# Twelve early gate/up units instead of eight, and GpSimd's FFN sums and low parts moved to VectorE, in a one-core transformer layer

## The chip, the core and the metric

One core of a Trainium2 chip runs the whole layer. TensorE (PE in the profile) multiplies, with its weight loads listed apart as PEld; VectorE (DVE), ScalarE (ACT) and GpSimd (POOL) do the work on elements; SyncE (SP) issues most DMAs. The metric is the device time of one execution in microseconds (us). The time before is the median of three runs.

## The reference

```
h = modulate(rms_norm(x, g_ffn1), sh_f1, sc_f1)
x = x + 0.5 * gt_f1 * ((silu(h @ w1_gu[gate]) * (h @ w1_gu[up])) @ w1_down)
h = modulate(rms_norm(x, g_mix), sh_m, sc_m);  z = h @ w_in     # two mixers: latent and grouped-query attention
x = x + gt_m * (concat(rms_norm(o_mla), rms_norm(o_gqa)) @ w_out)
h = modulate(rms_norm(x, g_ffn2), sh_f2, sc_f2)
x = x + 0.5 * gt_f2 * ((silu(h @ w2_gu[gate]) * (h @ w2_gu[up])) @ w2_down)
out = rms_norm(x, g_final)
```

All is float32, with 1024 tokens, a model width of 1024 and an FFN width of 2816. The nine vectors sh_*, sc_*, gt_* are the blocks of silu(c) @ w_ada + b_ada, each 1024 long.

## The kernel before

Every float32 operand of a matmul is split into a high part (ScalarE's cast, L105 or L461) and a low part (VectorE's subtraction, L106 or L462), and three matmuls on the parts replace one. So the FFNs are made of matmuls of 128x128 weights and 512 columns.

**Seven products.** Each FFN's gate/up projection uses a 2x2 block scheme with seven products instead of eight. The tokens are cut into two halves and the model width into two halves, which gives the blocks B11, B21 (first token half) and B12, B22 (second). `build` turns them into T1, T2, T3, T4 and the parts of B22, in eight steps (four 128-row chunks, two parts each); a step has four or five subtractions and low parts, of which GpSimd does one in the first part and three in the second. The weights come in 22 units (a gate and an up unit make a pair), each of four blocks A11, A12, A21, A22, streamed from DRAM, 1 MB a unit. `unit_specs` forms the sums S1 to S4 of the blocks: S1 and S3 on GpSimd, S2 and S4 on VectorE. A product is 12 matmuls (4 chunks, 3 terms).

**Early units.** A11xB11 and A12xB21 need the first token half alone. For the first NE units they run ahead of the rest, while the T blocks are still being built: the first NQ0 = 4 units in `early` (FFN1) or `early2` (FFN2), the others four at a time in `early_rest`. The weights of these two blocks come in transfers of their own (`first_spec`, one for a pair of units), and again with the unit. The result of A11xB11 (`c1`) and the first-half output (`ge_d`) go out to DRAM and come back in `run`. `run` then does five products for an early unit and seven for any other: A11, S2, S1, S3, A12, S4 and, one unit late, A22.

**What lies around the products.** `post` applies silu and the multiplication on the results, and `g_out` forms the sums S1 to S4 of the 512-wide results for the down projection, on GpSimd (L521), and stores them: names that begin with A on the SyncE queue, the others on GpSimd's. The down projection (`down`, L741 to L743) is again seven products, of 11 steps of 12 matmuls. Its first product takes the A12 results, loaded in three chunks.

**Streams and order.** `Stream.pump` splits the next weight blocks ahead of their use into a ring of nine units. After each product `tick` steps the background generators, pumps, and at `ada_rate` eighths of the ticks advances a second stream, `ada`: 56 steps that build seven of the nine modulation vectors, eight steps a vector. A step (L313) multiplies 128 rows of w_ada by c and adds them into the tile `acc`; there is one such tile at a time. When the eight steps of a vector are done, a generator sums `acc` over partitions with small matmuls (`mod_cols`, L328, or `mod_gate`, L342), and the next vector's memset waits for these. The rate is 0 in the early units of `run` and 5 in the others; what is left is done after it:

```
    ada.raw_pools["raw"] = (lambda: gup.tile([P, D], F32, tag="ada", name="ada", bufs=2), 2)
    ...
    ffn.run()
    while ada.i < len(ada.specs):
        ada.pump(1)
    bg.finish()
    gs.close()
    rs.close()
```

`gs.close()` gives back the pool of `acc`, `ada` and the results g; the tiles `gate` and x of the down projection take its place. PSUM tiles come from three pools of 3, 1 and 4 banks ("0", "1" and "2"), in rotation: in `run` by SIX = 0, 0, 0, 1, 2 low, 2 low; in `down` the eight accumulators take all banks, in the order 0, 0, 0, 1 for the first product and the four of pool 2 for the second.

The framework sets the order of each engine's queue when the program is built: code order counts first, but an instruction whose inputs it expects to be ready may go ahead of one that it expects to wait. On the chip each queue runs in its order.

Of the kernel before, what the change touches and what calls it, by code (L numbers as in the profile page):

```python
# [19 lines left out]
ALU = mybir.AluOpType  # L20
# [13 lines left out]
RING = 9  # L34
RAWB = 2
NQ0 = 4
NE = 8
TAIL = 3
YQ, YQ2, YL = 0, 1, 0
QB = 1  # L40
# [11 lines left out]
class Stream:  # L52
# [87 lines left out]
    def get(self, key):  # L140
        while key not in self.units:
            assert self.i <= self.where[key], key
            if self._next_is_block() and self.live >= RING:
                self.live -= self.freed
                self.freed = 0
                assert self.live < RING, key
            self._step()
        return self.units[key]
# [35 lines left out]
def encoder_layer(ctx: ExitStack, tc: tile.TileContext, a: dict, out: bass.AP):  # L184
    nc = tc.nc
# [10 lines left out]
    st = Stream(nc, rawp, ring)  # L196
# [17 lines left out]
    def t2(name, dt=F32):  # L214
        return tmp.tile([P, 512], dt, tag="t2", name=name, bufs=6)

    def small(n, name):
        return sm.tile([P, 16], F32, tag="small", name=name, bufs=20)[:, 0:n]
# [30 lines left out]
    g_d = {nm: dram.tile([P, NF // 2, 512], F32, name=f"g_{nm}") for nm in ("A11", "A12", "A22", "S1", "S2", "S3", "S4")}  # L249
    ge_d = dram.tile([NE // 2, P, 512], F32, name="ge_d")  # L250
    p1_d = dram.tile([NE, P, 512], F32, name="p1_d")
    gd = dram.tile([3, D], F32, name="gd")
# [27 lines left out]
    def ps1():  # L280

        if banks["pair"] is not None:
            p = banks["pair"][:, 512:1024]
            banks["pair"] = None
            return p
        kind = banks["kinds"][banks["n"] % len(banks["kinds"])]
        banks["n"] += 1
        if kind[0] == "2":
            p = ps2()
            if kind == "2":  # L290
                banks["pair"] = p
            return p[:, 0:512]
        return (p0p if kind == "0" else p1p).tile([P, 512], F32, tag="ps1", name="ps1")
# [122 lines left out]
    def unit_specs(i, u, early):  # L416

        src = a[f"w{i}_gu"][u // 2, u % 2]
        A = [slice(j * 512, (j + 1) * 512) for j in range(4)]
        tmps = {}  # L420

        def comb(nm, eng, x, y, op):
            def f(raw):
                tmps[nm] = sp.tile([P, 512], F32, tag="S", name="S")
                get = lambda v: tmps[v] if isinstance(v, str) else raw[:, A[v]]
                eng.tensor_tensor(tmps[nm], get(x), get(y), op=op)  # L426
            return f

        def blk(nm, v):
            if isinstance(v, str):  # L430
                return ((i, u, nm), None, lambda raw: tmps[v])
            return ((i, u, nm), A[v], None)

        direct = not early
        steps = [comb("S1", nc.gpsimd, 2, 3, ALU.add), comb("S3", nc.gpsimd, 0, 2, ALU.subtract)]
        if direct:
            steps.append(blk("A11", 0))
        steps += [comb("S2", nc.vector, "S1", 0, ALU.subtract), blk("S2", "S2"), blk("S1", "S1"), blk("S3", "S3")]
        if direct:
            steps.append(blk("A12", 1))  # L440
        steps += [comb("S4", nc.vector, 1, "S2", ALU.subtract), blk("S4", "S4"), blk("A22", 3)]
        return [(src, steps)]
# [3 lines left out]
    class GateUp:  # L446
# [17 lines left out]
        def build(self, hf, kk, part):  # L464

            b11, b21, b12, b22 = hf[0][:, kk, :], hf[0][:, kk + 4, :], hf[1][:, kk, :], hf[1][:, kk + 4, :]
            if part == 0:
                nc.gpsimd.tensor_tensor(b11, b12, b11, op=ALU.subtract)
                self.split_b("T1", kk, b11, nc.vector)
                nc.vector.tensor_tensor(b11, b22, b11, op=ALU.subtract)  # L470
                self.split_b("T2", kk, b11, nc.vector)
            else:
                nc.gpsimd.tensor_tensor(b12, b22, b12, op=ALU.subtract)
                self.split_b("T3", kk, b12, nc.vector)
                self.split_b("B22", kk, b22, nc.gpsimd)
                nc.vector.tensor_tensor(b21, b21, b11, op=ALU.subtract)
                self.split_b("T4", kk, b21, nc.gpsimd)

        def prod(self, p, u, wn, bn, kks, start, stop):
            wh, wl = st.get((self.i, u, wn))  # L480
# [31 lines left out]
        def g_out(self, fp, nm):  # L512

            g = self.g

            def put(nm):
                (nc.sync if nm[0] == "A" else nc.gpsimd).dma_start(g_d[nm][:, fp, :], g[nm])

            def comb(nm, x, y, op, into=None):
                g[nm] = gtp["g"]() if into is None else g[into]  # L520
                nc.gpsimd.tensor_tensor(g[nm], g[x], g[y], op=op)  # L521
                put(nm)

            if nm != "A21":
                put(nm)
            if nm == "A11":
                comb("S3", "A11", "A21", ALU.subtract)
            if nm == "A22":
                comb("S1", "A21", "A22", ALU.add, "A21")
                comb("S2", "S1", "A11", ALU.subtract, "A11")  # L530
                comb("S4", "A12", "S2", ALU.subtract, "A12")
# [6 lines left out]
        def load_p1(self, u):  # L538
            if u < NE:
                self.c1[u] = t2("c1")  # L540
                nc.sync.dma_start(self.c1[u], p1_d[u])
# [8 lines left out]
        def early_rest(self, builds):  # L550

            K4 = (0, 1, 2, 3)
            for u0 in range(NQ0, NE, 4):
                us = range(u0, u0 + 4)
                for u in us:
                    self.bank[u] = ps1()
                    self.prod(self.bank[u], u, "A11", "B11", K4, True, True)
                    self.store_p1(u)
                    next(builds, None)
                    st.pump(2)  # L560
                    bg.step()
                for u in us:
                    self.prod(self.bank[u], u, "A12", "B21", K4, False, True)
                    self.early_out(u)
                    next(builds, None)
                    st.pump(2)
                    bg.step()
            for _ in builds:
                pass
# [44 lines left out]
        def run(self):  # L614
# [4 lines left out]
            for u in range(NU):  # L619
                early = u < NE  # L620
                ada_rate[0] = 0 if early else 5
# [44 lines left out]
    def gu_specs(i):  # L666
        for u in range(NU):
            for src, steps in unit_specs(i, u, "rest" if u < NE else None):
                st.add(src, steps)
# [191 lines left out]
    x = [xs.tile([P, D], F32, name=f"x{t}") for t in range(NT)]  # L861
# [121 lines left out]
    x = [dp.tile([P, D], F32, name=f"x{t}") for t in range(NT)]  # L983
# [439 lines left out]
    for s in range(NQ + LAG + 3):  # L1423
        if s < NQ:
            i, t = divmod(s, NT)
            p = scores(i, t)
            nm = small(1, "nm")
            nc.vector.tensor_reduce(nm, p, axis=AX.X, op=ALU.max, negate=True)  # L1428
        b = s - LAG
        if 0 <= b < NQ:  # L1430
            g, e = divmod(b, 2)
# [50 lines left out]
    oT, x, hf = {}, {}, {}  # L1482
# [120 lines left out]
    x = [dp.tile([P, D], F32, name=f"z{t}") for t in range(NT)]  # L1603
# [127 lines left out]
```

## Time and profile before

| | us |
|---|---|
| median of 3 runs (2046.16 to 2048.94) | 2048.51 |
| the profiled execution | 2049.28 |
| its span, first to last instruction | 2047.5 |
| PE busy in the span | 1971.7 |
| DVE busy | 1540.1 |
| ACT busy | 973.4 |
| POOL busy | 483.7 |

The mean granted TensorE clock is 0.988 of full speed. In the profile, a row of the timeline gives the start, the duration, the engine, the line, the operation and its tiles; a figure in brackets is the engine's idle time before it and what ended that. FFN1's gate/up stage runs from the start to 497 us, its down projection to about 710, the mixers to about 1380, FFN2's gate/up stage to 1821 and its down projection to the end.

### The profile page before, as it was taken

How to read it: one execution, taken by the hardware profiler on the slowest of the kernel's cores; microseconds unless marked ns; L12 is line 12 of the kernel's file. 1: busy time of each engine (PE TensorE's matmuls, PEld its weight loads, DVE VectorE, ACT ScalarE, POOL GpSimd, SP SyncE). 2: the span in 40 equal slices, each digit the busy share in tenths (PEclk: the TensorE clock that was granted, in tenths of full speed). 3: DMA queues.
4: the chain of work that ended last, by engine and by line, in shares of the span. 5: the costliest groups of instructions: out<-in, count | busy, mean ns of one | idle time of the engine just before them, and what ended most of it. 6: DMA issues, size and time to landing. Idle time of an engine off the chain costs nothing. (4 is left out here: it accounts for less than half of the span.)

```text
span 2047.5 us, 28023 instructions
## 1 busy us (share of the span) xinstructions
PE 1971.7 (96%) x10301; PEld 1678.1 (82%) x10301; DVE 1540.1 (75%) x2381; ACT 973.4 (48%) x1865; POOL 483.7 (24%) x428
## 2 busy tenths in 40 slices
PE   6889999999999999999999999998999999999998
PEld 5678888887788888798989998996788888877886
DVE  7898689886697776788888778667776555547976
ACT  6522322322344653677787777467323333324444
POOL 1544344433000032212200000005343332320011
PEclk9999999999999999999999999998999999999999
DMA  8275366565832334523253330433442332358223
GB/s 344 88 246 186 106 202 216 197 223 187 334 116 93 147 123 143 156 63 118 89 165 83 83 75 30 164 127 126 165 163 100 113 118 83 113 207 322 98 93 118
DMA packets 90550, 303.30 MB, mean 148 GB/s; under 512 B 9848, under 2 KB 22427, under 8 KB 76588
## 3 DMA queue, kind: packets, MB, share of 16 engines
q1 hardware_dynamic: 81018, 274.21, 39.8%
q0 software_dynamic: 7040, 23.07, 2.9%
q10 hardware_dynamic: 2354, 4.22, 0.5%
q8 instruction: 81, 1.33, 0.3%
q14 instruction: 57, 0.47, 0.1%
HBM read 220.98 MB, written 80.49 MB: 147 GB/s over the span
## 5 line engine op out<-in xcount | busy, mean ns | idle before, releaser
L105 ACT CAST uh<-raw 128x512 fp32r<-128x512 f32 (+1 forms) x343 | 210.4, 622 | 228.8 <-PE ps L486 148.1
L106 DVE TENSOR_TENSOR ul<-raw,uh 128x512 fp32r<-128x512 f32 (+1 forms) x343 | 250.3, 735 | 41.1 <-ACT uh L105 40.7
L105 ACT CAST uh<-S 128x512 fp32r<-128x512 f32 x198 | 121.6, 621 | 302.3 <-PE ps L486 234.7
L741 PE MATMUL ps<-uh 128*128 128x512 f32 x616 | 240.8, 393 | 7.3 <-ACT uh L105 7.3
L742 PE MATMUL ps<-ul,uh 128*128 128x512 f32 x616 | 241.5, 392 | 1.7 <-DVE ul L106 1.7
L743 PE MATMUL ps<-uh,ul 128*128 128x512 f32 x616 | 240.9, 391 | 0.0
L1428 DVE TENSOR_REDUCE nm<-ps 128x1 f32<-128x1024 f32 x128 | 155.7, 1216 | 70.6 <-PE ps L223 40.9
L106 DVE TENSOR_TENSOR ul<-S,uh 128x512 fp32r<-128x512 f32 x198 | 168.8, 858 | 41.8 <-ACT uh L105 41.6
L521 POOL TENSOR_TENSOR g<-g 128x512 f32<-128x512 f32 x88 | 135.1, 1535 | 244.3 <-DVE g L508 243.3
L1446 ACT CAST ph<-ps 128x512 fp32r<-128x512 f32 x256 | 138.0, 590 | 79.6 <-PE ps L1445 79.4
L426 POOL TENSOR_TENSOR S<-raw 128x512 f32<-128x512 f32 x88 | 123.4, 1414 | 200.3 <-DMA raw<-in_w_gu_dram 122.5
L1456 DVE TENSOR_TENSOR pl<-ps,ph 128x512 fp32r<-128x512 f32 x256 | 163.9, 683 | 0.0
L1451 ACT ACTIVATE pe<-ps,nm 128x1024 f32<-128x1024 f32 x128 | 143.6, 1122 | 17.2 <-DVE nm L1428 17.1
L741 PEld LDWEIGHTS ps<-uh 128*128 128x128 f32 x616 | 116.1, 189 | 33.2 <-ACT uh L105 9.0
L742 PEld LDWEIGHTS ps<-ul,uh 128*128 128x128 f32 x616 | 116.4, 189 | 27.7 <-DVE ul L106 3.8
L743 PEld LDWEIGHTS ps<-uh,ul 128*128 128x128 f32 x616 | 116.3, 189 | 24.2
L1445 PE MATMUL ps<-ident,pe 128*128 128x128 f32 x1024 | 134.9, 273 | 0.8 <-DVE pl L1456 0.4
L1445 PEld LDWEIGHTS ps<-ident,pe 128*128 128x128 f32 x1024 | 119.7, 141 | 19.0 <-DVE pl L1456 0.6
L105 ACT CAST uh<-hT 128x512 fp32r<-128x512 f32 x96 | 59.7, 622 | 150.4 <-PE ps L742 113.5
L1394 PE MATMUL po<-ph,V 128*128 128x256 f32 x512 | 129.7, 291 | 0.0
L1395 PE MATMUL po<-pl,V 128*128 128x256 f32 x512 | 125.9, 283 | 0.0
L233 POOL TENSOR_TENSOR r<-v,neghalf 128x1 f32<-128x1 f32 x32 | 26.0, 813 | 363.8 <-DVE v L229 363.8
(280 smaller groups left out, 5178.0 us busy)
## 6 DMA issues: line engine op xcount, KB each, us to landing
raw<-in_w_gu_dram SPq DMA_DIRECT2D x52, 1024.0 KB
ada<-in_w_ada_dram SPq DMA_DIRECT2D x56, 512.0 KB
g_S<-g POOLq DMA_DIRECT2D x88, 256.0 KB, 2.6
g_A<-g SPq DMA_DIRECT2D x66, 256.0 KB
hT<-in_w_down_dram SPq DMA_DIRECT2D x16, 1024.0 KB
raw<-g_S SPq DMA_DIRECT2D x16, 1024.0 KB
raw<-g_A SPq DMA_DIRECT2D x12, 1024.0 KB
x<-in_x_dram SPq DMA_DIRECT2D x16, 512.0 KB
```

Of the source, the lines that this page charges most:

```text
L105: nc.scalar.copy(hi[:, 0:n], ap)
L106: nc.vector.tensor_tensor(lo[:, 0:n], ap, f32(hi[:, 0:n]), op=ALU.subtract)
L521: nc.gpsimd.tensor_tensor(g[nm], g[x], g[y], op=op)
L741: nc.tensor.matmul(p, gh[:, tsl], wh, start=start, stop=False, skip_group_check=True)
L742: nc.tensor.matmul(p, gh[:, tsl], wl, start=False, stop=False, skip_group_check=True)
L743: nc.tensor.matmul(p, gl[:, tsl], wh, start=False, stop=stop, skip_group_check=True)
L1394: nc.tensor.matmul(po[:, 0:256], V, gr.ph[:, k, :], start=(k == 0), stop=False)
L1428: nc.vector.tensor_reduce(nm, p, axis=AX.X, op=ALU.max, negate=True)
L1445: nc.tensor.transpose(out=pt[:, k, :], in_=pe[:, (4 * n + k) * P:(4 * n + k + 1) * P], identity=ident)
L1446: nc.scalar.copy(gr.ph[:, 4 * n:4 * n + 4, es], pt)
L1451: nc.scalar.activation(pe, p, AF.Exp, bias=nm, accum_out=ls[:, s % 2:s % 2 + 1])
L1456: nc.vector.tensor_tensor(gr.pl[:, nsl, es], pts[n], f32(gr.ph[:, nsl, es]), op=ALU.subtract)
```

## The change

NE goes from 8 to 12, so that `early_rest` does two groups of four units where it did one. The sums S1 and S3 of the weights, the four result sums of `g_out`, and in `build` the first subtraction of each part and the low parts of B22 and T4 go from GpSimd to VectorE. In `early_rest` the pump of the weight stream is put ahead of the next build step.

```diff
-NE = 8
+NE = 12
...
-        steps = [comb("S1", nc.gpsimd, 2, 3, ALU.add), comb("S3", nc.gpsimd, 0, 2, ALU.subtract)]
+        steps = [comb("S1", nc.vector, 2, 3, ALU.add), comb("S3", nc.vector, 0, 2, ALU.subtract)]
...
             if part == 0:
-                nc.gpsimd.tensor_tensor(b11, b12, b11, op=ALU.subtract)
+                nc.vector.tensor_tensor(b11, b12, b11, op=ALU.subtract)
...
             else:
-                nc.gpsimd.tensor_tensor(b12, b22, b12, op=ALU.subtract)
+                nc.vector.tensor_tensor(b12, b22, b12, op=ALU.subtract)
                 self.split_b("T3", kk, b12, nc.vector)
-                self.split_b("B22", kk, b22, nc.gpsimd)
+                self.split_b("B22", kk, b22, nc.vector)
                 nc.vector.tensor_tensor(b21, b21, b11, op=ALU.subtract)
-                self.split_b("T4", kk, b21, nc.gpsimd)
+                self.split_b("T4", kk, b21, nc.vector)
...
             def comb(nm, x, y, op, into=None):
                 g[nm] = gtp["g"]() if into is None else g[into]
-                nc.gpsimd.tensor_tensor(g[nm], g[x], g[y], op=op)
+                nc.vector.tensor_tensor(g[nm], g[x], g[y], op=op)
                 put(nm)
...
                     self.store_p1(u)
+                    st.pump(2)
                     next(builds, None)
-                    st.pump(2)
                     bg.step()
...
                     self.early_out(u)
+                    st.pump(2)
                     next(builds, None)
-                    st.pump(2)
                     bg.step()
```

## Rows read from the trace of the kernel before

**Rows 1.** The page's first part: busy us, share of the span, instructions.

```profile
PE 1971.7 (96%) x10301; PEld 1678.1 (82%) x10301; DVE 1540.1 (75%) x2381; ACT 973.4 (48%) x1865; POOL 483.7 (24%) x428
```

**Rows 2.** Windows by stretch: length, busy us (instructions) of each engine, PEclk, DMA, GB/s.

```profile
62.15:98.85 36.70, 29.72 (x121) 22.77 (x120) 34.18 (x35) 24.27 (x45) 21.78 (x14) 0.95 0.24 82
98.85:155.25 56.40, 49.76 (x205) 39.77 (x205) 51.61 (x60) 14.13 (x25) 24.43 (x20) 0.94 0.70 246
215.10:497.90 282.80, 282.49 (x1265) 232.06 (x1264) 221.31 (x269) 82.78 (x142) 110.28 (x87) 1.00 0.57 191
497.90:530.00 32.10, 28.10 (x113) 21.97 (x114) 19.36 (x27) 13.42 (x25) 6.55 (x7) 0.95 0.83 310
1396.60:1447.95 51.35, 41.02 (x157) 32.07 (x157) 46.46 (x44) 26.40 (x49) 33.22 (x21) 0.87 0.34 118
1447.95:1821.00 373.05, 372.85 (x1645) 308.38 (x1644) 225.38 (x320) 112.60 (x185) 128.78 (x119) 1.00 0.35 122
1821.00:1855.00 34.00, 29.52 (x119) 23.20 (x120) 20.38 (x28) 13.76 (x26) 6.54 (x7) 0.95 0.82 314
```

**Rows 3.** DVE's timeline in FFN2's early units.

```profile
1400.83 1.77 DVE L462 TENSOR_TENSOR T1l<-hT,T1h 128x512 fp32r<-128x512 f32 x1
...
1417.20 0.68 DVE L462 TENSOR_TENSOR T1l<-hT,T1h 128x512 fp32r<-128x512 f32 x1
1417.80 0.68 DVE L106 TENSOR_TENSOR ul<-raw,uh 128x512 fp32r<-128x512 f32 x1
...
1445.83 1.76 DVE L426 TENSOR_TENSOR S<-S,raw 128x512 f32<-128x512 f32 x1 [3.10 <-POOL S L426]
```

**Rows 4.** PE's timeline in the starts of FFN1 and FFN2.

```profile
147.34 0.80 PE L485 MATMUL ps<-T4h,uh 128*128 128x512 f32 x1 [4.10 <-DVE s L501]
...
1422.98 0.79 PE L485 MATMUL ps<-B21h,uh 128*128 128x512 f32 x1 [6.21 <-ACT c L493]
```

**Rows 5.** Groups by form, GpSimd's sums: xcount, busy us, mean ns, idle before.

```profile
L521 POOL TENSOR_TENSOR g<-g 128x512 f32<-128x512 f32 x88 | 135.1, 1535 | 244.3 <-DVE g L508 243.3
L426 POOL TENSOR_TENSOR S<-raw 128x512 f32<-128x512 f32 x88 | 123.4, 1414 | 200.3 <-DMA raw<-in_w_gu_dram 122.5 <-DVE ul L106 59.5 <-DVE g L508 9.6
```

**Rows 6.** The chain that ended last, FFN2's hand-over to its down projection.

```profile
1822.88 1.67 POOL g L521
...
1829.57 3.46 DMA g_S<-g
...
1833.36 0.33 SPq L397
...
1835.84 10.50 DMA raw<-g_A
```

**Rows 7.** PE's timeline at both hand-overs.

```profile
497.20 0.39 PE L487 MATMUL ps<-T4h,ul 128*128 128x512 f32 x1
497.95 1.20 PE L741 MATMUL ps<-uh 128*128 128x512 f32 x4 [0.37 <-ACT uh L105]
...
524.22 0.58 PE L741 MATMUL ps<-uh 128*128 128x512 f32 x1 [3.14 <-ACT uh L105]
...
525.61 0.63 PE L743 MATMUL ps<-uh,ul 128*128 128x512 f32 x1
526.04 0.63 PE L741 MATMUL ps<-uh 128*128 128x512 f32 x1
...
1847.62 0.50 PE L741 MATMUL ps<-uh 128*128 128x512 f32 x1 [3.32 <-ACT uh L105]
```

**Rows 8.** The ada stream by line: durations min/median/max ns, first and last start.

```profile
L313 DVE SCALAR_TENSOR_TENSOR acc<-ada,cact,acc x56: 1269/1277/2916, 122.0 to 469.7; 128x1024 f32<-128x1024 f32 x56
L342 PE MATMUL ps<-acc,ones x12: 591/592/592, 253.2 to 475.2; 128*128 128x512 f32 x12
```

**Rows 9.** Timeline of the ada stream's sixth and seventh vectors.

```profile
436.70 1.84 PE L328 MATMUL ps<-ones,acc 128*128 128x1 f32 x16
...
469.68 1.28 DVE L313 SCALAR_TENSOR_TENSOR acc<-ada,cact,acc 128x1024 f32<-128x1024 f32 x1
```

## The prediction

> **What bounds the kernel now.** The page's busy shares come first: PE is busy for 1971.7 of 2047.5 us, and no other engine for more than 75% [rows 1]. So only the time in which PE stands still or runs at the lower clock can be won, and I looked for it stretch by stretch. The windows show where it lies. In FFN2's steady products 1644 matmuls take 373.05 us, 0.227 us each and 2.72 us a product of 12, at full clock [rows 2]. By this pace (one matmul of each count reaches over the edge) the other windows lose:
>
> - FFN1's start, 62.15 to 98.85: 120 matmuls need 27.2 of 36.7 us, 9.5 lost. From 98.85 to 155.25, its first units of `run`: 204 need 46.3 of 56.4, 10.1 lost.
> - FFN2's start: 156 need 35.4 of 51.35, 16.0 lost; the granted clock is 0.87, so part is the 1.2 GHz level after idling.
> - The hand-overs to the down projections: 112 matmuls in 32.1 us lose 6.7 (FFN1), 118 in 34.0 lose 7.2 (FFN2).
>
> That is 49.5 us, and the reader is to see in the same rows that VectorE is busy for 90 to 93% of the three starts.
>
> **Why the starts lose.** VectorE's timeline shows the same operation on the same shape at 0.68 us and at 1.77 [rows 3]. The long ones fall where GpSimd runs a sum or a low part; in FFN2's start there are 19 of them, of which rows 3 show the first and the last. One follows another 0.60 us after its start when undisturbed. PE's waits are the result: 6.21 us for ScalarE's copy of a product, queued behind casts that wait for VectorE, and 4.10 us for a result that VectorE reads late [rows 4].
>
> **Part 1: GpSimd's work on VectorE.** Moved are 88 weight sums and 88 result sums [rows 5], and 4 instructions in each of 4 chunks of 2 FFNs, 32: 208 instructions at 0.60 us, 125 us of VectorE. In FFN2's start the 21 on GpSimd cost at most 12.6 us, and the 19 long ones give back 19 x 1.08 = 20.5, so VectorE gets about 8 us lighter there. In FFN1's run it gets 56 (14 units: two sums a unit, four a pair), 34 us on 221 of 283: 90% if no long one shortened. I put that at nothing, under PE's products; were VectorE full, its excess would be PE's loss.
>
> This rests on the contention, so the Trainium skill is weighed here. The Trainium skill, SBUF — State Buffer, section "Who interferes with whom", says that a VectorE instruction with two SBUF inputs and a GpSimd instruction that reads SBUF block each other for the whole instruction; the two durations in rows 3 agree. The Trainium skill, Perfetto Trace Analysis, section "Optimizing Scalar/DVE Operations", has the rule against the change: where VectorE is saturated, move work off it, even to GpSimd, though it adds that between these two it may not help. Its outcome is the last rival below.
>
> A new wait: a sum on VectorE now waits itself for the unit's weights, for which GpSimd waited 122.5 us [rows 5], with low parts and `post` queued behind. But S2 on VectorE followed GpSimd's S1 already (3.10 us of waiting in the last of rows 3), and gets ready two GpSimd sums (2.8 us) sooner. I take nothing; a sum that waits longer than PE's lead of split units would cost its excess.
>
> **Part 2: four more early units.** PE's products stay the same in number. Eight of them, 21.8 us, move from `run` to the start of each FFN and cover the T builds. Each FFN has about 5 MB more to move (two 1 MB transfers, four results and two pairs of outputs out and back), with some ten more issues on SP and four on ScalarE's queue. DMA is busy for 0.24 and 0.34 of the starts [rows 2], so this is hidden; if not, at 314 GB/s it is 16 us an FFN. The pump ahead of the build step only orders VectorE's queue in PE's favour.
>
> What comes back: VectorE's own work in FFN1's start, 34.2 us plus 14 GpSimd instructions and the splits of the moved products (8.4 + 6), fits into 36.7 + 21.8 us even without relief. Of the 19.6 us lost there I take 13: the first eight ada steps, which ran from 122.0 [rows 8] among the first units and not where the code pumps them, still press on VectorE. Of FFN2's 16.0 I take 12. The bounds are nothing and all.
>
> **Part 3: FFN2's hand-over.** PE waits for the third chunk of A12 results. Followed back, its load waits on SP behind the gate and x loads, and these for the last sum's store [rows 6]. Between the first sum's start and that store's issue lie 6.7 us; three sums of 0.60 and 0.4 for the store make 2.2. All comes 4.5 us sooner, more than PE's wait of 3.32 [rows 7]. With it go nine matmuls at 0.43 instead of 0.227 us (1.2 GHz, as rows 7 show after FFN1's wait), 1.8 us: 5 us. Bounds 0 and 7.2.
>
> **Part 4: FFN1's hand-over, where the change costs.** The ada stream advances only in units that are not early. `run` has 4 ticks in the first unit, 5 in other early ones, 7 in the rest and one at the end. Before: ticks 39 to 138, 62 pumps for 56 steps, done in time (the last step starts at 469.7, its sums end at 475.8, rows 8; PE ends `run` at 497.4, rows 7). After: ticks 59 to 130, floor(650/8) - floor(295/8) = 45. Eleven steps are left for the loop after `run`: the end of the sixth vector and all of the seventh.
>
> Call T the end of `run` on PE. The fifth vector's sums come at tick 124, six products before T: 16.3 us and their own 1.9, T - 18.2. From such sums to the end of the next vector's eighth step it took 436.70 to 470.96, 34.3 us [rows 9], so the sixth is ready at T + 16.1, its matmuls end at T + 17.9 and their bank is read at about T + 18.4. The rotation decides who waits: 48 + 50 products and 7 tiles of earlier vectors make the sixth's tile number 105, which is pool 1's only bank, and the first down product needs that bank in its first step. PE can do nine matmuls (2.0 us) before it, and the 1.8 us of sums were spent earlier before: 18.4 - 3.8 = 14.6 lost, and 1.8 at the lower clock. The seventh vector is ready at T + 50.4; its two tiles hold pool 2, which the second down product needs, and the first is free at about T + 52 (four matmuls of 0.59, rows 8, and a copy). PE comes there at T + 18.4 + 27.9 + 1.8 = T + 48.1: some 3 us more. In exchange the third chunk has long landed. Lost are 19.4 instead of 7.1 (with the 0.37 us of rows 7): +12. Bounds: -5, if all hides as in FFN2, and +39, the fourth case below.
>
> **Sum.** 2049.3 - 13 - 12 - 5 + 12 = 2031.3 by the profiled execution, which is 0.8 above the median of the runs: **2031**. Own range 2021 to 2043.
>
> **The cases.**
> 1. As summed, chance 0.48.
> 2. The ada tail hides: other banks, or its steps run further ahead, as the first eight did. Against it: `acc` is one tile, so a vector can't start before the sums of the last. -13 - 12 - 5 - 5: 2014, chance 0.17.
> 3. The starts give back half: the queues' order keeps ScalarE's copies behind casts that wait for VectorE [rows 4]. -12.5 - 5 + 12: 2043, chance 0.12.
> 4. Slower, by the pool's release. The gate and x loads wait for the pool that holds `acc`, so until about T + 54; if the third chunk's load stands behind them on SP, as in rows 6, it lands 2.5 + 10.5 us later, at T + 67, and PE, at its ninth step at T + 40, waits 28 us more. Lost are 46 in place of 7: -30 + 39, 2058. It decides from a loss of 37 us on. For it: that order stands in the trace. Against it: the loads' places were chosen by expected readiness, and these are now expected late. Chance 0.15.
> 5. VectorE becomes the bound: without relief FFN1's two stretches ask 85.8 + 20.4 + 6 of 114.9 us, 98%, and nothing comes back in the starts. -5 + 12: 2056, chance 0.08. The rule of the Trainium skill (Perfetto Trace Analysis, above) on moving work off a full VectorE has this outcome.
>
> About 0.2% (4 us) can be told from no change. Case 1, case 2 and half of case 3 are faster by more, less a little for case 1's edge: 0.67; 0.12 the same; 0.21 slower. The range, 2012 to 2056, takes in cases 1, 2, 3 and 5 and leaves out the fourth and the edges of the others.
>
> **What would show it.** Right: no VectorE instruction of 1.7 us in the gate/up stages, FFN2's start without the 6.21 us wait, FFN2's hand-over without the 3.32; at the end of FFN1's `run`, L313 steps after PE's last product and PE idle for some 14 us before its first down step. Wrong: PE goes straight into the down projection (case 2), or stops again at the ninth step (case 4), or VectorE is as full in the starts as before (cases 3 and 5).

## The result and the profile after

The changed kernel takes 2012.12 us (median of 4 runs, 2009.51 to 2014.59) where the kernel before, on the same chip, took 2048.73 (4 runs, 2046.16 to 2049.21): a ratio of 0.9824, 95% interval 0.9807 to 0.9841. That is 36.6 us less, twice the 17.5 of the forecast: below the 2021 to 2043 of its first case, and 0.1 us inside the range of all cases, 2012 to 2056. The profiled execution took 2012.8 us, its span is 2011.0.

The page's busy shares, which answer to [rows 1]:

```profile
PE 1959.4 (97%) x10301; PEld 1674.1 (83%) x10301; DVE 1557.2 (77%) x2589; ACT 975.9 (49%) x1865; POOL 171.5 (9%) x220
```

The 208 instructions stand on VectorE (2381 to 2589) and have left GpSimd (428 to 220). VectorE's busy time has hardly risen, by 17.1 us, where 208 x 0.60 are 125: the rest came back as shorter instructions.

The windows by stretch, as in [rows 2] with the stages at their new times; the first is the whole of 62.15 to 155.25, which was two rows there:

```profile
62.15:155.25 93.10, 93.10 (x410) 76.13 (x409) 84.17 (x131) 44.94 (x80) 3.32 (x5) 1.00 0.66 226
214.00:470.90 256.90, 256.90 (x1151) 211.97 (x1149) 206.21 (x297) 74.90 (x124) 19.91 (x33) 1.00 0.55 183
470.90:500.00 29.10, 22.15 (x87) 17.77 (x87) 22.26 (x32) 9.96 (x18) 3.13 (x5) 0.82 0.81 275
1385.40:1436.70 51.30, 51.30 (x226) 41.83 (x225) 41.26 (x67) 30.31 (x55) 0.00 (x0) 1.00 0.53 180
1436.70:1792.00 355.30, 354.77 (x1565) 293.45 (x1565) 249.96 (x392) 106.29 (x174) 22.25 (x41) 1.00 0.39 134
1792.00:1826.00 34.00, 34.00 (x151) 28.14 (x151) 22.06 (x37) 16.19 (x30) 1.63 (x3) 1.00 0.93 358
```

In FFN1's start PE does 409 matmuls of 0.227 us in 93.1 us, so it loses 0.3 where it lost 19.6; in FFN2's start 225 in 51.3, 0.2 where it lost 16.0. VectorE does 131 instructions in 84.2 us where it did 95 (35 and 60) in 85.8, and 67 in 41.3 where it did 44 in 46.5: more instructions in less time. FFN2's hand-over (last row) loses nothing. FFN1's (third row) is the one that got worse, with a granted clock of 0.82.

VectorE's timeline in FFN2's early units, as [rows 3]: the low part of T1 and those around it take 0.68 or 0.69 us each and follow one another every 0.60.

```profile
1384.48 0.68 DVE L473 TENSOR_TENSOR hT<-hT 128x512 f32<-128x512 f32 x1
1385.08 0.68 DVE L106 TENSOR_TENSOR ul<-raw,uh 128x512 fp32r<-128x512 f32 x1
1385.68 0.68 DVE L462 TENSOR_TENSOR T1l<-hT,T1h 128x512 fp32r<-128x512 f32 x1
```

In the whole trace 114 of VectorE's 128x512 operations on two inputs took over 1 us before, each of them beside a GpSimd instruction; 5 do after. PE's waits of [rows 4] are gone: neither of the two starts has a wait of PE.

FFN1's hand-over, PE's timeline, in place of the first part of [rows 7] (between the first row and the second PE does nothing else):

```profile
470.70 0.39 PE L487 MATMUL ps<-T4h,ul 128*128 128x512 f32 x1
475.69 1.65 PE L741 MATMUL ps<-uh 128*128 128x512 f32 x3 [4.60 <-ACT uh L105]
...
481.97 0.40 PE L743 MATMUL ps<-uh,ul 128*128 128x512 f32 x1
484.71 1.95 PE L328 MATMUL ps<-ones,acc 128*128 128x1 f32 x16 [2.35 <-DVE acc L313]
486.52 1.29 PE L741 MATMUL ps<-uh 128*128 128x512 f32 x4
487.61 0.63 PE L742 MATMUL ps<-ul,uh 128*128 128x512 f32 x1
...
515.56 1.98 PE L342 MATMUL ps<-acc,ones 128*128 128x512 f32 x4 [1.29 <-DVE acc L313]
...
549.59 1.20 PE L741 MATMUL ps<-uh 128*128 128x512 f32 x4 [2.01 <-ACT uh L105]
```

The end of `run` on PE, T, is 470.93. The reader sees the ada tail: the sixth vector's sums (L328) and the seventh's (L342) stand among down products, and PE waits for both. VectorE's last step of the sixth vector waited itself for its load, and VectorE's next two low parts for the down products stand behind it and behind the copy that reads the sums:

```profile
483.38 1.28 DVE L313 SCALAR_TENSOR_TENSOR acc<-ada,cact,acc 128x1024 f32<-128x1024 f32 x1 [3.21 <-DMA ada<-in_w_ada_dram]
484.58 0.69 DVE L106 TENSOR_TENSOR ul<-raw,uh 128x512 fp32r<-128x512 f32 x1
486.70 0.17 DVE L331 COPY modB<-ps 128x8 f32<-128x8 f32 x1 [1.43 <-PE ps L328]
486.78 0.68 DVE L106 TENSOR_TENSOR ul<-hT,uh 128x512 fp32r<-128x512 f32 x1
```

FFN2's hand-over has one wait, of 0.53 us, in place of the 3.32 of [rows 7], and the first down product follows the last gate/up product (1790.58) at once:

```profile
1791.27 1.20 PE L741 MATMUL ps<-uh 128*128 128x512 f32 x4 [0.53 <-ACT uh L105]
```

**Where the time went, stage by stage.** For this kernel and each one below I counted what PE loses, as the prediction did: the length of a stretch less 0.227 us for each matmul of 512 columns in it. "FFN1" is from 40 us to the end of `run`, and includes what the ada vectors' own matmuls take above that pace (8.0 us where seven are summed there, 5.9 for five); "FFN2" is from its first B21 product to the end of its `run`; a hand-over is the 90 us after that. "Long" counts VectorE's 128x512 operations over 1 us. The stages are read from one profiled execution of each kernel, which can lie some us from its median: 2044.92 us for e1, 2018.08 for e5. The names are explained in the experiments.

| kernel | median us | ratio, 95% | FFN1 | hand-over | FFN2 | hand-over | long |
|---|---|---|---|---|---|---|---|
| before | 2048.73 | | 41.1 | 7.0 | 16.0 | 7.5 | 114 |
| changed | 2012.12 | 0.9807-0.9841 | 16.2 | 18.1 | 0.4 | 0.7 | 5 |
| e1_cover_alone | 2047.93 | 0.9986-1.0004 | 30.4 | 18.8 | 10.5 | 7.2 | 112 |
| e2_vector_alone | 2001.23 | 0.9753-0.9782 | 21.2 | 0.7 | 0.0 | 0.7 | 6 |
| e3_old_pump | 2015.16 | 0.9821-0.9851 | 17.4 | 17.2 | 0.3 | 0.7 | 6 |
| e4_ada_in_early | 2000.20 | 0.9744-0.9776 | 20.8 | 0.7 | 0.6 | 0.7 | 5 |
| e5_vectors_in_pool2 | 2015.69 | 0.9831-0.9861 | 18.8 | 19.9 | 0.7 | 0.7 | 5 |
| e6_builds_alone | 2023.49 | 0.9867-0.9896 | 30.5 | 5.6 | 1.2 | 7.7 | 91 |
| e7_weight_sums_alone | 2041.67 | 0.9964-0.9984 | 37.3 | 6.3 | 11.7 | 8.4 | 80 |
| e8_result_sums_alone | 2034.97 | 0.9926-0.9956 | 39.3 | 0.7 | 15.9 | 0.7 | 66 |
| e9_ada_faster_late | 2014.19 | 0.9819-0.9849 | 34.6 | 0.9 | 0.5 | 0.7 | 6 |
| e10_gpsimd_for_nobody | 2039.02 | 0.9941-0.9971 | 41.6 | 0.7 | 17.9 | 0.7 | 38 |
| e11_eight_early | 2001.13 | 0.9756-0.9786 | 21.7 | 0.7 | 0.0 | 0.7 | 5 |
| e12_four_early | 2028.09 | 0.9892-0.9925 | 38.2 | 0.7 | 10.2 | 0.7 | 6 |

From before to changed the four stretches sum to -24.9 + 11.1 - 15.6 - 6.8 = -36.2 us; the span went down by 36.5. So nothing of size happened elsewhere.

### The profile page after: what moved, and what is told of

Same layout as the page of the kernel before. It is cut to its first block, busy times and chain, and to the rows that moved or that the text cites. A ratio compares the mean times of both kernels' runs of the same rounds, so it can differ in the third digit from the quotient of the medians.

```text
span 2011.0 us, 27995 instructions
## 1 busy us (share of the span) xinstructions
PE 1959.4 (97%) x10301; PEld 1674.1 (83%) x10301; DVE 1557.2 (77%) x2589; ACT 975.9 (49%) x1865; POOL 171.5 (9%) x220
## 4 chain that ended last, share of the span: by engine, by line
PE 91%; DVE 3%; ACT 2%; DMA 1%; issue 1%; POOL 0%; POOLq 0%; SPq 0%; ACTq 0%; DVEq 0%
PE ps L485 14%; PE ps L486 14%; PE ps L487 14%; PE ps L741 6%; PE ps L742 6%; PE ps L743 6%; PE ps L1445 5%; PE ps L221 5%; PE ps L223 5%; PE ps L222 5%; PE po L1394 3%; PE po L1395 3%; PE ps L1378 1%; PE ps L1379 1%; DMA ada<-in_w_ada_dram 1%
## 5 line engine op out<-in xcount | busy, mean ns | idle before, releaser
L106 DVE TENSOR_TENSOR ul<-raw,uh 128x512 fp32r<-128x512 f32 (+1 forms) x343 | 234.5, 690 | 29.1 <-ACT uh L105 28.8
L106 DVE TENSOR_TENSOR ul<-S,uh 128x512 fp32r<-128x512 f32 x198 | 135.3, 684 | 30.8 <-ACT uh L105 30.8
L1451 ACT ACTIVATE pe<-ps,nm 128x1024 f32<-128x1024 f32 x128 | 143.7, 1122 | 17.1 <-DVE nm L1428 16.9
L517 POOL DMA_DIRECT2D g_S<-g x88 | 47.9, 544 | 681.4 <-DVE g L521 587.6
L1394 PEld LDWEIGHTS po<-ph,V 128*128 128x128 f32 x512 | 97.5, 190 | 2.1
L1395 PEld LDWEIGHTS po<-pl,V 128*128 128x128 f32 x512 | 97.8, 191 | 0.2
```

Source lines behind the costliest of these rows:

```text
L106: nc.vector.tensor_tensor(lo[:, 0:n], ap, f32(hi[:, 0:n]), op=ALU.subtract)
L1394: nc.tensor.matmul(po[:, 0:256], V, gr.ph[:, k, :], start=(k == 0), stop=False)
L1395: nc.tensor.matmul(po[:, 0:256], V, gr.pl[:, k, :], start=False, stop=(k == NT - 1))
```

## The experiments

Each was timed in turns with the kernel before on its chip, and the ratio is against that: a median of 2048.55 for e1 to e4, 2047.50 for e5 to e8, 2048.31 for e9 to e12.

**The two halves of the change, each alone.** `e1_cover_alone` is the kernel before with twelve early units; `e2_vector_alone` is the changed kernel with eight, and with the pump at its old place.

```diff
(e1, against before)      (e2, against changed)
-NE = 8                   -NE = 12
+NE = 12                  +NE = 8
```

> Twelve early units alone; GpSimd keeps its sums and low parts, and the pump stays behind the build step. Both starts lost 35.8 us of PE time before and 1.0 after the whole change; FFN1's hand-over lost 7.0 and then 15.1 without the two vectors' own matmuls. Contention theory (VectorE was late because GpSimd's instructions lengthen its own to 1.7 us): the long instructions stay, the starts keep 25 us or more of their loss, the ada tail adds 8 to 12: 2046 to 2052. Cover theory (PE ran out of products while the T blocks were built): the eight moved products bring nearly all back, 2049 - 33 + 10 = 2026.

> Eight early units as before, but all of GpSimd's sums and low parts on VectorE; the pump stays behind the build step. No ada step is left for the end of FFN1's run. Contention theory: no VectorE instruction of 1.7 us, the starts give back 25 to 33, both hand-overs 6 each: 2004 to 2012, as fast as the whole change or faster. Cover theory: VectorE is still the later engine while the T blocks are built, the starts give back under 10, the hand-overs 12: 2027 or more.

VectorE alone gives 47 us, more than the whole change and 3 us past what was expected; the twelve units alone give nothing that can be told from zero. The table says why. In e1 the starts give back 10.7 (of which 2.1 is only two vectors' sums moved out) and 5.5 us, with 112 long instructions still there, and FFN1's hand-over takes 11.8. In e2 FFN2's start and both hand-overs give back nearly everything, FFN1's start all but some 2 of its 19.6 us, and no tail is left over.

**The pump's place.** `e3_old_pump` is the changed kernel with the pump behind the build step.

```diff
-                    st.pump(2)
                     next(builds, None)
+                    st.pump(2)
```

> The whole change without the swapped lines in early_rest: the pump stands behind the build step. If the order of these two lines does nothing, because the builds are done by the second unit of the first group, 2012 and the starts lose 1 us. If it is what keeps PE fed, the starts lose 5 us or more and it takes 2017 or more.

2015.16 against 2012.12 with overlapping intervals, and stages that agree within 1.2 us: undecided here. With eight units the same edit is nothing (`e11_eight_early` below, 2001.13 against 2001.23).

**The tail taken away.** `e4_ada_in_early` is the changed kernel with two eighths, not none, as the ada rate of the early units.

```diff
-                ada_rate[0] = 0 if early else 5
+                ada_rate[0] = 2 if early else 5
```

> The whole change, with the ada stream at 2 eighths of the ticks in early units of run in place of 0: 14 more steps there, so all 56 are done before run ends. Tail theory: FFN1's hand-over loses under 1 us as FFN2's does, in place of 15, so 1996 to 2000. Rival: VectorE gets full in the early units (17.5 instructions of 0.60 us and 1.25 steps of 1.2 in 13.6 us, 88%) and PE waits there: the run of FFN1 loses 5 us or more, 2003 or more.

2000.20 us, 12 less. The 56 steps are done in `run`, and PE goes into the down projection after 0.32 us:

```profile
L313 DVE SCALAR_TENSOR_TENSOR acc<-ada,cact,acc x56: 1273/1280/1286, 104.3 to 460.8; 128x1024 f32<-128x1024 f32 x56
```
```profile
477.62 1.20 PE L741 MATMUL ps<-uh 128*128 128x512 f32 x4 [0.32 <-ACT uh L105]
```

The hand-over loses 0.7 in place of 18.1, of which 4.6 us appear again in FFN1's stage, 2.1 of them as the two vectors' own matmuls. So the tail's cost is shown, and it is what separates the change from its VectorE half.

**The tail's mechanism.** `e5_vectors_in_pool2` gives the vectors' sums, in both of their generators, a tile of pool 2, which the first down product does not need, in place of pool 1's only bank.

```diff
-        p = ps1()
+        p = ps2()[:, 0:512]
```

> The whole change, but the small matmuls that end an ada vector write into a PSUM tile of pool 2 instead of the next one in the rotation. Bank theory: the first down product's fourth accumulator no longer waits for the sixth vector, so FFN1's hand-over loses 7 us or less until the second product, which still waits for the seventh vector's pool 2 tiles; that second wait ended 45 us after run and PE reaches it 6 us sooner: hand-over 12 to 15 in place of 18, 2007 to 2010. Rival: PE's queue itself holds the small matmuls ahead of the down steps, and they wait for the ada steps whatever bank they use: the same 2012.

No gain: 2015.69, and the hand-over loses 19.9. PE's timeline of e5:

```profile
477.78 1.20 PE L741 MATMUL ps<-uh 128*128 128x512 f32 x4 [3.56 <-ACT uh L105]
...
486.70 1.92 PE L328 MATMUL ps<-ones,acc 128*128 128x1 f32 x16 [1.39 <-issue]
488.48 0.48 PE L742 MATMUL ps<-ul,uh 128*128 128x512 f32 x1
...
518.32 1.98 PE L342 MATMUL ps<-acc,ones 128*128 128x512 f32 x4 [3.00 <-DVE acc L313]
```

The order of PE's matmuls says why. In the changed kernel the sums stand behind 18 down matmuls of three accumulators (475.69 to 481.97 above); with the bank freed they stand behind 22 of four accumulators, and still ahead of the fourth accumulator's next matmuls (488.48), which need nothing of them. So the bank kept four matmuls behind the sums, 0.9 us of work. With either bank the sums stand in PE's way. Their place is not shown to be all that holds PE, though: VectorE's queue has the next step's low parts behind the same late ada step and behind the copy of the sums (484.58 and 486.78 in the changed kernel, 486.52 and 488.74 in e5), so PE would soon have stopped for them. Neither queue's order was changed by itself.

**Which of GpSimd's three works.** Each alone on VectorE, the rest as before, with eight units: the T builds, the weight sums S1 and S3, the result sums.

```diff
(e6)  -  nc.gpsimd.tensor_tensor(b11, b12, b11, ...)   + nc.vector...   (and the other three of a chunk)
(e7)  -  comb("S1", nc.gpsimd, ...), comb("S3", nc.gpsimd, ...)   + nc.vector
(e8)  -  nc.gpsimd.tensor_tensor(g[nm], g[x], g[y], op=op)   + nc.vector...
```

> The kernel before, with only the T blocks' work (16 instructions an FFN) moved to VectorE. Contention theory: the long VectorE instructions of the two starts go with GpSimd's builds, but the weight sums still lengthen some: FFN2's start loses 2 to 6 us of its 16, FFN1's start and first units 18 to 24 of 31, both hand-overs their 7: 2022 to 2030. Rival (the weight sums are what made PE wait): FFN2's start keeps 10 or more, 2035 or more.

> The kernel before, with only the weight sums S1 and S3 (88 instructions) moved to VectorE. Contention theory: the builds' 16 GpSimd instructions an FFN still lengthen VectorE's in the starts, so FFN2's start keeps 8 to 12 of 16; FFN1's first units of run lose less: 2035 to 2042. Rival: the sums' own lateness was what PE waited for, FFN2's start loses under 4, 2030 or less.

> The kernel before, with only the result sums (88 instructions) moved to VectorE. Hand-over theory: both hand-overs lose 1 in place of 7, the starts keep their loss as no result sum runs in them: 2049 - 12 = 2035 to 2038. Rival (the hand-overs won because all stages ran lighter): under 6 us won, 2043 or more.

Against 2047.50 for before: 24.0, 5.8 and 12.5 us, 42.3 in sum of the 47 together. They act in different places. The 32 instructions of the builds, the fewest, give over half: 10.6 us in FFN1's start and 14.8 in FFN2's, and little at the hand-overs (7.0 to 5.6, and 7.5 to 7.7). The weight sums give 3.8 and 4.3 in the starts. The result sums give nothing in FFN2's start (15.9 of 16.0 are still lost), and nearly all at the two hand-overs, 6.3 and 6.8: the wait of Part 3, and the same at FFN1's hand-over (how it goes is told under Part 3 below).

**Contention or lateness?** All this could come from GpSimd's results being late, not from what its reading does to VectorE. `e10_gpsimd_for_nobody` is e2 with 32 GpSimd subtractions more, whose output nobody reads.

```diff
                 self.split_b("T4", kk, b21, nc.vector)
+                for nm in ("T3", "B22", "T4", "T1"):
+                    nc.gpsimd.tensor_tensor(b12, f32(self.Bh[nm, kk]), b12, op=ALU.subtract)
```

> The kernel with all of GpSimd's work on VectorE and eight early units (2001.2 us, six VectorE instructions over 1 us), plus four subtractions of 128x512 on GpSimd in each of the four steps of the build's second part, 16 an FFN, which read T3, B22, T4 and T1 and write a buffer that nobody reads: nothing on VectorE, ScalarE or PE waits for a result of them. The dead buffer is given back later, which is the only other tie. Theory of contention (GpSimd's reading lengthens VectorE's instructions): some 16 more VectorE instructions over 1 us in each FFN, each about 1.1 us longer, 17 us an FFN of VectorE's time in its fullest stretch; PE loses again 5 to 12 us in each start, and the time is 2008 to 2025. Rival (GpSimd's own lateness was what PE waited for, and the long VectorE instructions only stood beside it): the time stays at 2001 within 4 us. A time that stays although long instructions are in the trace would say that VectorE had room for them.

2039.02 us, 38 more than e2 and above my bounds. GpSimd's and VectorE's timelines in FFN2's start:

```profile
1419.09 1.72 POOL L479 TENSOR_TENSOR hT<-T4h,hT 128x512 f32<-128x512 f32 x1
1420.77 1.74 POOL L479 TENSOR_TENSOR hT<-B22h,hT 128x512 f32<-128x512 f32 x1
1422.47 1.74 POOL L479 TENSOR_TENSOR hT<-T1h,hT 128x512 f32<-128x512 f32 x1
```
```profile
1419.60 1.76 DVE L476 TENSOR_TENSOR hT<-hT 128x512 f32<-128x512 f32 x1
1421.28 1.78 DVE L462 TENSOR_TENSOR T3l<-hT,T3h 128x512 fp32r<-128x512 f32 x1
1422.98 1.77 DVE L462 TENSOR_TENSOR B22l<-hT,B22h 128x512 fp32r<-128x512 f32 x1
```

They run one to one: one VectorE instruction of 1.7 us for each of GpSimd's. There are 38 long ones in place of 6, 32 more for 32 added, and no wait of VectorE in that start names GpSimd. The windows of the two FFN2 starts, e10 and then e2:

```profile
1391.00:1474.00 83.00, 70.46 (x289) 56.52 (x288) 77.50 (x100) 34.87 (x63) 28.23 (x17) 0.90 0.36 125
```
```profile
1371.00:1437.00 66.00, 66.00 (x293) 54.62 (x292) 61.66 (x102) 34.77 (x63) 1.16 (x2) 1.00 0.47 158
```

VectorE's hundred instructions take 15.8 us more for 16 of GpSimd's, and the start takes 17.0 us longer for some 290 matmuls. VectorE was full there (61.7 of 66 us), so each microsecond that it was held became one of PE's. Contention is shown, by itself, without lateness. That lateness cost nothing in the kernel before is not shown: in its two starts VectorE waited 4.2 and 3.1 us for GpSimd's weight sums (the last of [rows 3] is one such wait), about what e7 gains there.

**How much cover is needed.** `e11_eight_early` and `e12_four_early` are the changed kernel with eight and four early units.

```diff
-NE = 12
+NE = 8      (e11)     NE = 4      (e12)
```

> The changed kernel with eight early units in place of twelve, so GpSimd's work on VectorE and the pump ahead of the build step. Main theory, that the twelve units bring nothing but the tail, and that the pump's place is worth nothing here: 2001, as with the old order (2001.2). Rival, that the pump ahead of the build step lets PE's weights through first, as the 3 us between the changed kernel with and without it may say: 1998.

> The changed kernel with four early units in place of twelve: nothing but the first four units covers the building of the T blocks. Theory that a relieved VectorE needs no more cover: FFN1 and FFN2 lose no more than with eight, the tail is gone (more ticks at five eighths), and the time is about 2000. Rival, that cover is still needed: the early products are then 8, 21.8 us, and four of the eight steps of a build, some 8 to 9 VectorE instructions of 0.6 us each, 20 us in all, stand between them and PE's next product; PE waits 5 to 15 us in each start, and the time is 2010 to 2030.

Eight units are enough, 2001.13, the same as e2. Four are not, 2028.09, though only six long instructions are left: FFN1 loses 16.5 us more than with eight, FFN2 10.2. VectorE alone is the bound there; windows of the two starts of e12, and a wait of PE in the first:

```profile
40.00:117.00 77.00, 59.90 (x249) 47.09 (x249) 72.71 (x120) 41.83 (x73) 1.70 (x2) 0.87 0.39 137
1386.70:1440.50 53.80, 47.34 (x193) 38.03 (x193) 51.93 (x87) 27.53 (x50) 0.62 (x1) 0.94 0.37 124
```
```profile
83.31 0.80 PE L487 MATMUL ps<-T2h,ul 128*128 128x512 f32 x1 [9.73 <-DVE ul L106]
```

**Another way to be rid of the tail.** `e9_ada_faster_late` keeps ada out of the twelve units and raises it to seven eighths in the ten others.

```diff
-                ada_rate[0] = 0 if early else 5
+                ada_rate[0] = 0 if early else 7
```

> The changed kernel with the ada stream at seven eighths of the ticks, not five, in the ten units of `run` that are not early (still none in the early twelve): 71 x 7/8 = 62 pumps, enough for the 56 steps, nearly all in the last 192 us of the stage. Main theory, by which the tail is all that the twelve early units cost and VectorE has room: the changed kernel's VectorE is busy for 154.8 us of the last 192.5 us of its run at five eighths; seven eighths add at most 17 steps of 1.28 us, 22 us, so 177 of 192.5, 92%. It holds; the hand-over loses about 1 us in place of 18, and the time is about 2000, as with the stream in the early units. Rival, VectorE full: by unit 7 x 7/8 steps are 7.8 us on top of some 10.7, 18.5 of 19.0, and with the waits for weights and results in its queue that is over the limit; PE then waits in these ten units, by 5 to 15 us, and the time is 2005 to 2015.

2014.19: the hand-over is cured (0.9), and FFN1's stage gives all of it back, 34.6 in place of e4's 20.8. The time lies in the rival's range, but not by its cause, a full VectorE. Windows and PE's waits of those units:

```profile
298.00:490.60 192.60, 185.44 (x805) 149.73 (x803) 156.18 (x210) 49.29 (x85) 14.38 (x22) 0.96 0.65 218
```
```profile
PE ps L328 <- DVE acc L313: 3.7, 3, 1.8
PE ps L485 <- DVE s L501: 2.5, 2, 2.1
PE ps L342 <- DVE acc L313: 1.0, 1, 1.0
```

VectorE is busy for 81%, and its steps waited 10.6 us in that stretch for ada loads. PE stands still for 7.2 us, 4.7 of them for vectors' sums that are not ready at their place in its queue, as in the tail; the granted clock of 0.96 makes, as an estimate, 192.6 x 0.04 = 7.7 us more. So it is the tail's wait four times over, between products. That this rate makes the loads late, and not the framework's placing alone, wasn't tried apart.

The fastest are e4, e11 and e2, at 2000 to 2001, which these intervals don't tell apart. The simplest of them is the VectorE half alone.

## Why the prediction came out as it did

The direction was right, and so was the contention behind the starts; the size of what comes back was not, and the two hand-overs went in part another way than forecast. By its own terms:

| term | forecast | measured (from the table) |
|---|---|---|
| FFN1's start | -13 | -22.8 (-24.9, less 2.1 of sums only moved) |
| FFN2's start | -12 | -15.6 |
| FFN2's hand-over | -5 | -6.8 |
| FFN1's hand-over | +12 | +9.0 (11.1 less the same 2.1) |
| sum | -18 | -36.2 |

**The step that failed** is Part 2's "What comes back". It took 13 of 19.6 and 12 of 16.0 us, and 0.3 and 0.2 are left in those windows; another 2.7 came from before 62 us (11.0 lost there before, 8.3 after) and 0.8 from behind 155, which the forecast did not count. Of the 18.2 us between forecast and result, 13.4 lie in this step, 3.0 in FFN1's hand-over and 1.8 in FFN2's. The caution had one ground, and it didn't hold: the first eight ada steps do fall in the same place (104 to 130 us), but VectorE had room for them once relieved. For FFN2's 12 of 16 it gave none. And the forecast's own bound, that VectorE's work fits "even without relief", was read as one outcome among several; e10 and e12 show what it was, the condition that decides: with VectorE's work fitting in, next to nothing is lost, and past that about every microsecond is. A partial return is what one gets when the condition fails in part, as in e1 and e7, and there was no reason in the rows for that here. The busy share does not show the condition: VectorE is busy for 92% of FFN1's start before, with 19.6 us lost, for 90% in the changed kernel, with 0.3 lost, and for 97% in e2 (90.6 of the same 93.1 us), with some 2 lost. So one of the forecast's signs of being wrong, a VectorE "as full in the starts as before", would have misled in that start.

**Part 1** held. The long instructions are gone, and the 208 cost 17.1 us of VectorE's busy time in place of 125. The Trainium skill, SBUF — State Buffer, section "Who interferes with whom", describes the exclusive lock; e10 agrees, with one VectorE instruction of 1.7 us for each GpSimd instruction. The excess in FFN1's `run`, costed at nothing, was nothing (206.2 of 256.9 us busy, 80%). Of the fifth case and the rule beside it the last clause was the right one: the Trainium skill, Perfetto Trace Analysis, section "Optimizing Scalar/DVE Operations", says that moving work off a saturated VectorE, even to GpSimd, may make sense, and warns that between these two engines it might not help. Here the reverse move relieved the full engine.

**Part 2's premise**, that the moved products cover the builds, was right for before (e1: the starts gain 14 us without the two vectors' sums), but little of it is left on top of Part 1: e2, with eight units, loses 2.9 us more in FFN1's stage than the changed kernel (21.2, less 2.1 for two vectors more, against 16.2) and no more in FFN2's. The two remedies were for the same loss, and the forecast priced its return once, under the cover, where the relief alone brings nearly all.

**Part 3** came near by its number, 6.8 for 5, but not by its way. The sums are quicker: 3.5 us from the start of the first of the last three (1793.19) to the last store's issue (1796.69), where it was 6.7. But the gate load, which waits for that store, starts no sooner: 13.9 us after the end of `run` (1790.58), before 12.6 (1833.36 in [rows 6], after 1820.80). What changed is SyncE's order. The third chunk's load now stands ahead of the gate and x loads, 6.9 us after the end of `run` where it was 15.0 (1835.84):

```profile
1797.51 0.33 SPq L95 DMA_DIRECT2D raw<-g_A  x1
1804.50 0.33 SPq L397 DMA_DIRECT2D gate<-gd  x1
```

In e8 this load stands ahead of the gate's at both hand-overs, so the new order comes with the result sums, and FFN1's hand-over had the same 6.3 to give, which the ada tail hid. Why the framework set it so, no run shows.

**Part 4** held in its counting. Eleven steps were left. The fifth vector's sums began at T - 18.2 as forecast, the sixth's at T + 13.8 (forecast T + 16.1), the seventh's at T + 44.6 (T + 50.4), the last two with PE waiting. Freeing the bank gained nothing, though (e5), and PE did not idle some 14 us before its first down step: it waited 4.60 us for the first down weights, did 18 matmuls ahead of the sums and not nine, and then waited 2.35. SyncE's queue has the load of these weights (467.50) behind ada's:

```profile
459.44 5.77 SPq L95 DMA_DIRECT2D ada<-in_w_ada_dram  x3
465.48 0.33 SPq L517 DMA_DIRECT2D g_A<-g  x1
467.07 0.33 SPq L95 DMA_DIRECT2D ada<-in_w_ada_dram  x1
467.50 0.38 SPq L729 DMA_DIRECT2D hT<-in_w_down_dram  x1
```

Its issue is 3.4 us before T, where before it was 5.2, and ScalarE's first cast of the weights starts 7.5 us after the issue (475.01), where before it took 5.1 (492.18 to 497.28). That the order of the loads is what made this one late was not tried apart from the tail, and the cause of the 2.01 us wait at 549.59, which e5 has too (2.00), stays open. Of the 18.1 us lost here PE's waits for the sums are 3.6; the two other waits are 6.6, and both are gone with the tail in e4.

**The other cases.** Case 2, 2014, is nearest by its number and wrong by its mechanism: the tail did not hide. Case 3, half given back, is refuted by the windows. Case 4 did not occur: SyncE's loads of A12 results stand ahead of the gate's,

```profile
498.03 0.38 SPq L95 DMA_DIRECT2D raw<-g_A  x1
...
509.75 0.42 SPq L95 DMA_DIRECT2D raw<-g_A  x1
...
519.00 0.34 SPq L397 DMA_DIRECT2D gate<-gd  x1
```

and PE had no wait between the seventh vector's sums and 549.59. Case 5 is what e12 shows with four units, not with twelve.

## What to carry to other kernels

Where VectorE's timeline shows one operation at two durations, look which GpSimd instructions lie beside the long ones: moving these onto the crowded engine can empty it, and the worth is the full loss of the stretch as soon as its own work fits, not a share. Look at the loss and not at the busy share, which can be as high where the loss is gone. Two remedies for one loss don't add, and each brings its own cost; try each alone. A background stream whose rate hangs on the number of steps of one kind must be counted again when that number changes, and where queues run in a fixed order, a late sum can hold what stands behind it in PE's queue and behind its reader in VectorE's, even when its buffer is changed.

## What was not expected of the hardware

The price of a GpSimd instruction that nobody needs: 32 of them, about 1.7 us each, made the kernel 38 us slower, 1.2 us each, though GpSimd was otherwise nearly idle (1.16 us busy in that 66 us stretch of e2). The forecast's 1.08 us for a lengthened VectorE instruction was near this price, and it was paid in full in the two starts, where VectorE was full.
